# 39 rows of the gather stage get their dot products on TensorE

## The chip, the cores and the metric

One core of a Trainium2 chip runs the whole program: TensorE (matrix products, transposes), VectorE, ScalarE, GpSimd ("Pool", which here issues the indirect transfers) and SyncE (which issues the other transfers), with 16 transfer engines behind the queues. The metric is the device time of one execution in microseconds, as a median of runs.

## The reference

One layer on 256 tokens of width 2048, all in float32: a mixer of block attention and gated linear attention, a cross attention over 256 memory tokens, and a feed-forward part made of single experts, each with a layer norm behind it. The change lies in the feed-forward part:

```python
q = (xt @ w_query).reshape(T, PEER_HEADS, 2, PEER_QUERY_DIM // 2)
s = jnp.einsum('thpd,hpnd->thpn', q, sub_keys).astype(jnp.float32)
s_top, i_top = lax.top_k(s, PEER_TOPK)
...
best, pos = lax.top_k(cand, PEER_TOPK)
expert_idx = jnp.take_along_axis(cand_idx, pos, axis=-1)
gates = jax.nn.softmax(best, axis=-1)
...
u = expert_down[idx]
h = jax.nn.gelu(jnp.einsum('td,thkd->thk', xc, u).astype(jnp.float32), approximate=False)
vsel = expert_up[idx]
return jnp.einsum('thk,thkd->td', (g * h).astype(x.dtype), vsel)
```

So each of 256 tokens picks 16 of 16384 experts in each of 8 heads. Of each expert it needs one row of 2048 numbers of the table `peer_u` (expert_down) for a dot product with the token, and one of `peer_v` (expert_up) for the weighted sum.

## The kernel before

The tokens are two halves, s = 0 and s = 1, of 128 tokens, one to a partition. For each half and each of 8 x 16 = 128 slots there is thus one "row" of work: an indirect transfer (`gather`, L660) that fetches for each of 128 tokens its own expert's row of `peer_u`, 128 x 2048 float32 or 1.049 MB, and then a dot product of each partition's row with its token (`dot` in `u_row`, L669): one VectorE operation over 128 x 2048 with an accumulator, which writes one column of `z`. The last part of the kernel handles `peer_v` another way for most slots: it streams the whole table through TensorE against a matrix of weights that is built from one-hot tiles (`one_hot`, `weigh_hot`, `build`), block by block of tokens (IB = 4 tokens to a block).

`KS = (128, 75)` says how many slots of each half are gathered in the gather stage: all 128 of s = 0 and the first 75 of s = 1, 203 rows. The other 53 slots of s = 1 are left to the last part of the kernel, whose order is written by hand and is not touched.

The gather stage (`run`, L895 to L928) goes head by head. `peer_scores(h0, 2, h2)` computes the queries of two heads on TensorE (L200, from four tiles of `peer_wq`, tag "wr", 1 MB each), ScalarE copies them (`pq`, L204), TensorE multiplies them with the keys (L574). `route(s, h)` (L606 to L650) is the selection of the 16 experts: chains of maximum, find and replace operations on VectorE, an index computation (L629 to L642), and a softmax of the gate (ScalarE's exponential at L647, VectorE's reciprocal at L649). `gather_u(s, heads)` then issues a head's 16 gathers and dots; `weigh` (L684, L685) applies the Gelu and the gates to a head's 16 columns of `z`. In s = 1 the builds of 64 blocks run between the heads: for one block `one_hot` and `weigh_hot` write one-hot tiles (four VectorE operations of 128x128 at L744, called hot-row operations here, the rest on ScalarE at L731 and L733), TensorE multiplies them (L753), and ScalarE copies the result out (L756).

A gather needs a free slot. For s = 0 there are nine: three of the pool `g`, two halves of `h2s`, and four of `gslots`; for s = 1 there are six: three of `g` and three buffers "gw" of the tag "wr", which held the weight tiles before. A slot is free when the dot that reads it has run, so Pool's next gather waits for an earlier dot. The transfers then run on the queue of Pool.

There are two kinds of PSUM banks: `pp` (five) and `pa` (three). The order of the instructions in this stage isn't written out by hand: a scheduler sets the order of each engine from the priorities (the order in which the program is written) and from its own estimate of when each operand is ready. `tc.issue_after(x)` binds what is written under it to come after instruction x.

Of the kernel before, what the change touches and what calls it, by code (L numbers as in the profile page):

```python
# [7 lines left out]
F32 = mybir.dt.float32  # L8
# [4 lines left out]
ALU = mybir.AluOpType  # L13
# [3 lines left out]
P = 128  # L17
T = 256
D = 2048
KT = 16  # L20
# [5 lines left out]
PH = 8  # L26
NK = 128
TK = 16
# [23 lines left out]
TB = 4  # L52
LNC = ((0, 2, 0, 2), (0, 2, 0, 2))
SG = 8


class Body:
# [477 lines left out]
    def sub_keys(self):  # L535
        nc = self.nc
        src = self.A["peer_sub_keys"][0].rearrange("h s n d -> n (h s) d")
        self.skT = self.sm.tile([P, 2 * PH, P], F32, name="skT", bufs=1)
        tiles = []
        for g in range(4):  # L540
            t = self.sm.tile([P, 4, P], F32, name=self.name("sk"), tag="f2", bufs=4)
            nc.sync.dma_start(t, src[:, g * 4:(g + 1) * 4, :])
            tiles.append(t)
        self.sk_finish(self.sk_transpose(tiles[:2], "pa"))
        return tiles[2:]
# [107 lines left out]
    def gather(self, table, s, i):  # L653
# [8 lines left out]
            in_offset=bass.IndirectOffsetOnAxis(ap=self.eidx[:, s, i:i + 1], axis=0))  # L662
        return g

    def u_row(self, s, i):
        g = self.gather(self.A["peer_u"][0], s, i)

        def dot():
            self.nc.vector.scalar_tensor_tensor(g, g, 1.0, self.h2n[:, s, :], op0=ALU.mult, op1=ALU.mult,  # L669
                                                accum_out=self.z[:, s, i:i + 1])  # L670
        return dot

    def v_row(self, s, i):
# [13 lines left out]
    def gather_u(self, s, heads):  # L687
        for h in heads:
            lo, hi = h * TK, min((h + 1) * TK, KS[s])
            for i in range(lo, hi):  # L690
                self.u_row(s, i)()
            self.weigh(s, lo, hi)

    def residual(self):
# [149 lines left out]
    def run(self):  # L844
        A, nc, tc, ctx = self.A, self.nc, self.tc, self.ctx
# [25 lines left out]
        with tc.tile_pool(name="smR", bufs=2) as self.sm:  # L871
# [10 lines left out]
            h2 = h2s[:, 0:2, :].rearrange("p a (k t) -> p (a k) t", t=T)  # L882
# [14 lines left out]
            self.slots = spare  # L897
            self.gather_u(0, (0,))
            self.slots = spare + [lambda k=k: gs[:, k, :] for k in range(4)]
            todo = [(1,)]  # L900
            for h0 in (2, 4, 6):
                self.peer_scores(h0, 2, h2)
                for h in (h0, h0 + 1):
                    self.route(0, h)
                self.gather_u(0, todo.pop(0))
                todo.append((h0, h0 + 1))
            for h in range(2):
                self.route(1, h)
            self.gather_u(0, todo.pop(0))
# [104 lines left out]
```

## Time and profile before

| | us |
|---|---|
| median of 3 runs | 2262.85 (2260.82 to 2269.27) |
| the profiled execution | 2258.22 |
| its span in the trace | 2256.5 |
| VectorE busy in the span | 1717.4 |
| TensorE busy in the span | 1748.3 |

The trace is of one execution, and a sum over its rows is held against that execution's own 2258.22 us. In the gather stage the rows are numbered here 0 to 127 (s = 0) and 128 to 202 (s = 1), in order of their gathers; the first dot of row 48, which is head 3 of s = 0, starts at 1020.13 us, the first of s = 1 at 1248.82, and the last of them ends at about 1473.7. Heads are given as (s, head): head (0, 3) to (0, 7), then (1, 0) to (1, 4), whose last has 11 rows.

In rows of instructions the columns are the start and the duration in us, the engine, the line, the operation, output and inputs by the program's names, shapes, how many in a run, and in brackets the idle time ahead with what ended it. "PEclk" is TensorE's clock as granted, as a share of 2.4 GHz (0.50 is 1.2 GHz).

### The profile page before, as it was taken

The page shows a single profiled execution, that of the slowest core. Times are in us where ns is not written, and L with a number is a line of the kernel's source. Part 1 is how long each engine was busy: PE and PEld are TensorE (multiplying, and loading weights), DVE is VectorE, ACT ScalarE, POOL GpSimd, SP SyncE. Part 2 cuts the span into 40 slices and gives each one's busy share as a digit, 9 for nine tenths or more (in the row PEclk, how much of TensorE's full clock was granted, in tenths as well). Part 3 has the DMA queues.
Part 4 walks back from the last instruction along what each step waited for, and adds up shares of the span by engine and source line. Part 5 has one row for each costly group of instructions (what it writes and reads, how often), then busy time and mean ns, then how long its engine had stood idle before and what let it go on. Part 6 is the DMA issues. An engine that isn't in the chain of part 4 may idle for free.

```text
span 2256.5 us, 22663 instructions
## 1 busy us (share of the span) xinstructions
PE 1748.3 (77%) x8238; PEld 1454.3 (64%) x8238; DVE 1717.4 (76%) x2382; ACT 905.0 (40%) x1408; POOL 493.4 (22%) x348
## 2 busy tenths in 40 slices
PE   8999999899999979840000551069999999999995
PEld 7778887788888868630000440068888887888884
DVE  5456555754444458989999999898888887899886
ACT  4554544444444431203100561074444444444443
POOL 0000000100000004522376336901222221222211
PEclk9999999999999989875555555589999999999998
DMA  6554558455545729999999999959999998999992
GB/s 226 176 162 156 168 168 279 136 195 192 188 148 192 254 96 375 422 376 322 312 379 383 337 314 332 395 185 326 355 375 373 361 356 326 378 386 362 363 377 93
DMA packets 160783, 637.47 MB, mean 283 GB/s; under 512 B 12304, under 2 KB 24720, under 8 KB 103968
## 3 DMA queue, kind: packets, MB, share of 16 engines
q1 hardware_dynamic: 116176, 312.01, 38.9%
q0 software_dynamic: 44496, 324.03, 37.8%
q8 instruction: 64, 1.05, 0.2%
q14 instruction: 47, 0.39, 0.0%
HBM read 628.65 MB, written 7.34 MB: 282 GB/s over the span
## 4 chain that ended last, share of the span: by engine, by line
PE 68%; DVE 20%; DMA 6%; issue 4%; POOL 2%; ACT 1%; SPq 0%; ACTq 0%; DVEq 0%; POOLq 0%
PE pp L183 9%; PE pp L819 6%; PE pp L821 6%; PE pp L818 6%; PE pp L218 6%; PE pp L219 6%; PE pp L217 5%; PE pp L185 5%; DVE g L669 5%; PE pa L821 4%; PE pa L819 4%; PE pa L818 4%; DMA wr<-in_peer_wq_dram 3%; DVE oh L744 3%; DVE gslots L669 3%
## 5 line engine op out<-in xcount | busy, mean ns | idle before, releaser
L152 DVE TENSOR_TENSOR wl<-wr,wh 128x1024 fp32r<-128x1024 f32 x512 | 623.1, 1227 | 411.0 <-ACT wh L151 410.7
L151 ACT CAST wh<-wr 128x1024 fp32r<-128x1024 f32 x512 | 537.8, 1052 | 692.3 <-PE pa L821 347.5
L669 DVE SCALAR_TENSOR_TENSOR g<-g,y 128x2048 f32<-128x2048 f32 x138 | 316.6, 2304 | 12.2 <-DMA g<-in_peer_u_dram,eidx 12.2
L660 POOL DMA_INDIRECT g<-in_peer_u_dram,eidx x138 | 208.9, 1514 | 425.7 <-DVE g L669 343.6
L819 PE MATMUL pp<-wl,ah 128*128 128x512 f32 x640 | 251.8, 393 | 2.6 <-DVE wl L152 2.6
L818 PE MATMUL pp<-wh,ah 128*128 128x512 f32 x640 | 250.5, 391 | 3.6 <-issue 2.8
L821 PE MATMUL pp<-wh,al 128*128 128x512 f32 x640 | 209.8, 393 | 0.0
L720 PE MATMUL pa<-ident,w 128*128 128x128 f32 x2 | 0.9, 462 | 209.0 <-DVE w L685 209.0
L819 PE MATMUL pa<-wl,ah 128*128 128x512 f32 x384 | 150.1, 391 | 0.0
L818 PE MATMUL pa<-wh,ah 128*128 128x512 f32 x384 | 150.0, 391 | 0.0
L819 PEld LDWEIGHTS pp<-wl,ah 128*128 128x128 f32 x640 | 120.6, 188 | 30.7 <-DVE wl L152 4.1
L818 PEld LDWEIGHTS pp<-wh,ah 128*128 128x128 f32 x640 | 120.4, 188 | 30.7 <-issue 2.9
L821 PEld LDWEIGHTS pp<-wh,al 128*128 128x128 f32 x640 | 120.5, 188 | 25.9
L183 PE MATMUL pp<-x,wh 128*128 128x512 f32 x384 | 136.3, 398 | 0.0
L720 PEld LDWEIGHTS pa<-ident,w 128*128 128x128 f32 x2 | 0.4, 183 | 209.7 <-DVE w L685 205.1
L660 POOL DMA_INDIRECT g<-in_peer_v_dram,eidx x53 | 72.7, 1372 | 263.9 <-DVE y L678 235.0
L821 PE MATMUL pa<-wh,al 128*128 128x512 f32 x384 | 129.6, 392 | 0.0
L720 PE MATMUL pa<-ident,ij 128*128 128x128 f32 x4 | 1.3, 434 | 161.3 <-DVE ij L641 161.3
L678 DVE SCALAR_TENSOR_TENSOR y<-g,w,y 128x2048 f32<-128x2048 f32 x53 | 124.4, 2347 | 0.0
L669 DVE SCALAR_TENSOR_TENSOR gslots<-gslots,y 128x2048 f32<-128x2048 f32 x48 | 109.7, 2301 | 0.0
L185 PE MATMUL pp<-x,wl 128*128 128x256 f32 x384 | 108.5, 283 | 0.0
L200 PE MATMUL pp<-h2s,wr 128*128 128x256 f32 x384 | 92.0, 401 | 17.6 <-DMA wr<-in_peer_wq_dram 17.6
(293 smaller groups left out, 3708.3 us busy)
## 6 DMA issues: line engine op xcount, KB each, us to landing
wr<-in_peer_v_dram SPq DMA_DIRECT2D x128, 1024.0 KB, 7.6
wr<-in_w_in_dram SPq DMA_DIRECT2D x48, 1024.0 KB, 5.1
wr<-in_xattn_wkv_dram SPq DMA_DIRECT2D x32, 1024.0 KB, 5.3
wr<-in_w_out_dram SPq DMA_DIRECT2D x16, 1024.0 KB, 5.2
wr<-in_xattn_wq_dram SPq DMA_DIRECT2D x16, 1024.0 KB, 4.9
wr<-in_xattn_wo_dram SPq DMA_DIRECT2D x16, 1024.0 KB, 4.9
wr<-in_peer_wq_dram SPq DMA_DIRECT2D x12, 1024.0 KB, 16.9
spill<-stg SPq DMA_DIRECT2D x16, 320.0 KB, 2.8
```

The lines of the kernel that those rows point to most:

```text
L151: self.nc.scalar.copy(wh, raw)
L152: (eng or self.nc.vector).tensor_tensor(wl, raw, wh.bitcast(F32), op=ALU.subtract)
L183: nc.tensor.matmul(ps[j], wh[:, k, c], xhl[:, k0 + k, :], start=(first and k == 0), stop=False, skip_group_check=True)
L185: nc.tensor.matmul(ps[j][:, :T], wl[:, k, c], xhl[:, k0 + k, 0:T], start=False, stop=(last and k == WK - 1), skip_group_check=True)
L218: nc.tensor.matmul(ps[h], xh, wl[:, k, :], start=False, stop=False)
L219: nc.tensor.matmul(ps[h], xl, wh[:, k, :], start=False, stop=(last and k == WK - 1))
L660: self.nc.gpsimd.indirect_dma_start(out=g, out_offset=None, in_=table, in_offset=bass.IndirectOffsetOnAxis(ap=self.eidx[:, s, i:i + 1], ax ...
L669: self.nc.vector.scalar_tensor_tensor(g, g, 1.0, self.h2n[:, s, :], op0=ALU.mult, op1=ALU.mult, accum_out=self.z[:, s, i:i + 1])
L678: self.nc.vector.scalar_tensor_tensor(acc, g, self.w[:, s, i:i + 1], acc, op0=ALU.mult, op1=ALU.add)
L818: nc.tensor.matmul(o, ah[th], wh[:, c, :], start=first, stop=False)
L819: nc.tensor.matmul(o, ah[th], wl[:, c, :], start=False, stop=False)
L821: nc.tensor.matmul(out[th][cp * WK + c], al[th], wh[:, c, :], start=False, stop=last)
```

## The change

In heads (0, 3) to (0, 7) the rows with i % 16 in (1, 4, 7, 10), and in heads (1, 0) to (1, 4) those with i % 16 in (0, 4, 8, 11), no longer get a dot on VectorE: 20 + 19 = 39 rows. The row is gathered as before. Then (`pe_row`) TensorE transposes its 16 pieces of 128x128 in four groups of four into a `pa` bank, ScalarE copies each group to a tile `gT` (two buffers), and TensorE multiplies each transposed piece with the same piece of the transposed tokens and adds over the 16 pieces in a `pp` bank: 16 float32 products of 128x128x128. The bank then holds the product of every token with every token's expert row; the wanted dots are its diagonal. VectorE takes that by a 128x128 operation with the identity and the accumulator (L685 after). This operation is bound behind the dot of a row three or more later, or of the head's last row.

For s = 1 the transposed tokens have to outlast `h2`, since its buffer becomes one of the next stage's; ScalarE copies the half to `h2b`, in the buffer of the keys `skT`, which get a tag for it. The diff:

```diff
 SG = 8
+PD = ((1, 4, 7, 10), (0, 4, 8, 11))
+PD0 = 3
+PL = 3
...
         src = self.A["peer_sub_keys"][0].rearrange("h s n d -> n (h s) d")
-        self.skT = self.sm.tile([P, 2 * PH, P], F32, name="skT", bufs=1)
+        self.skT = self.sm.tile([P, 2 * PH, P], F32, name="skT", tag="skT", bufs=1)
         tiles = []
...
+    def pe_row(self, s, i):
+        nc = self.nc
+        g = self.gather(self.A["peer_u"][0], s, i)
+        out = self.bank()
+        for c in range(4):
+            ps = self.bank("pa")
+            for j in range(4):
+                k = 4 * c + j
+                nc.tensor.transpose(ps[:, j * P:(j + 1) * P], g[:, k * P:(k + 1) * P], self.ident)
+            gT = self.sm.tile([P, 4, P], F32, name=self.name("gT"), tag="gT", bufs=2)
+            nc.scalar.copy(gT, ps.rearrange("p (a t) -> p a t", a=4))
+            for j in range(4):
+                k = 4 * c + j
+                nc.tensor.matmul(out[:, :P], gT[:, j, :], self.h2T[s][:, k, :], start=k == 0, stop=k == KT - 1)
+
+        def diagonal():
+            dg = self.sm.tile([P, P], F32, name=self.name("dg"), tag="s0", bufs=2)
+            nc.vector.scalar_tensor_tensor(dg, out[:, :P], 1.0, self.ident, op0=ALU.mult, op1=ALU.mult,
+                                           accum_out=self.z[:, s, i:i + 1])
+        return diagonal
+
     def u_row(self, s, i):
...
         def dot():
-            self.nc.vector.scalar_tensor_tensor(g, g, 1.0, self.h2n[:, s, :], op0=ALU.mult, op1=ALU.mult,
-                                                accum_out=self.z[:, s, i:i + 1])
+            return self.nc.vector.scalar_tensor_tensor(g, g, 1.0, self.h2n[:, s, :], op0=ALU.mult, op1=ALU.mult,
+                                                       accum_out=self.z[:, s, i:i + 1])
         return dot
...
             lo, hi = h * TK, min((h + 1) * TK, KS[s])
+            pend = []
             for i in range(lo, hi):
-                self.u_row(s, i)()
+                if i % TK in PD[s] and (s, h) >= (0, PD0):
+                    pend.append((i + PL, self.pe_row(s, i)))
+                    continue
+                dot = self.u_row(s, i)()
+                while pend and (pend[0][0] <= i or i == hi - 1):
+                    with self.tc.issue_after(dot.ins):
+                        pend.pop(0)[1]()
             self.weigh(s, lo, hi)
...
             self.slots = spare + [lambda k=k: gs[:, k, :] for k in range(4)]
+            self.h2T = [h2[:, :, 0:P], None]
             todo = [(1,)]
...
                 todo.append((h0, h0 + 1))
+            h2b = self.sm.tile([P, KT, P], F32, name="h2b", tag="skT", bufs=1)
+            nc.scalar.copy(h2b, h2[:, :, P:T])
+            self.h2T[1] = h2b
             for h in range(2):
```

The 203 gathers keep their order on Pool, and SyncE's order stays. The order of the other engines is set anew. In the pieces below pp, pa are PSUM banks with a running number, ident the identity, gslots, g, gw, h2s slots of gathered rows or `h2`, wr a weight tile, oh the one-hot tiles, dg the diagonal's output.

TensorE where the scores of heads 6 and 7 of s = 0 are computed, before: the queries follow the scores of heads 4 and 5 at once.

```order
L574 MATMUL pa_6975<-skT,pq_6883 128x128 x2
L200 MATMUL pp_7149<-h2s,wr_7147 128x256 x8
L200 MATMUL pp_7158<-h2s,wr_7147 128x256 x8
L200 MATMUL pp_7149<-h2s,wr_7167 128x256 x8
L200 MATMUL pp_7158<-h2s,wr_7167 128x256 x8
```

And after, the same place: the last of head 3's four rows ends in it (L676 transposes, L681 products).

```order
L681 MATMUL pp_7266<-h2s,gT_7283 128x128 x4
L676 MATMUL pa_7289<-ident,gslots 128x128 x2
L676 MATMUL pa_7300<-ident,gslots 128x128 x4
L203 MATMUL pp_7333<-h2s,wr_7331 128x256
L681 MATMUL pp_7266<-h2s,gT_7294 128x128 x4
L681 MATMUL pp_7266<-h2s,gT_7305 128x128 x4
L203 MATMUL pp_7333<-h2s,wr_7331 128x256 x7
L203 MATMUL pp_7342<-h2s,wr_7331 128x256 x8
```

The queries of heads 6 and 7 (L203 is L200 of before) have moved behind the four rows of head 3.

TensorE in head 2 of s = 1, before: nothing but products of one-hot tiles, one block after the other.

```order
L720 MATMUL pa_7578<-ident,w 128x128
L753 MATMUL pp_7687<-oh_7677 128x128 x4
L753 MATMUL pa_7704<-oh_7694 128x128 x4
L753 MATMUL pp_7721<-oh_7711 128x128 x4
L753 MATMUL pp_7738<-oh_7728 128x128 x4
```

After, the same engine from the third group of that head's last row on (L784 is L753 of before):

```order
L676 MATMUL pa_9546<-ident,g_9510 128x128 x4
L784 MATMUL pp_9585<-oh_9575 128x128
L681 MATMUL pp_9512<-h2b,gT_9540 128x128 x4
L681 MATMUL pp_9512<-h2b,gT_9551 128x128 x4
L784 MATMUL pp_9585<-oh_9575 128x128 x3
L784 MATMUL pa_9602<-oh_9592 128x128 x4
L784 MATMUL pp_9619<-oh_9609 128x128 x4
L784 MATMUL pa_9636<-oh_9626 128x128 x4
L784 MATMUL pp_9653<-oh_9643 128x128 x4
L784 MATMUL pp_9670<-oh_9660 128x128 x4
L784 MATMUL pa_9687<-oh_9677 128x128 x4
L676 MATMUL pa_9740<-ident,gw_9737 128x128 x4
```

The builds of seven blocks now stand together between the head's last row and the next head's first.

VectorE in the same head, before: after each dot one block's four hot-row operations.

```order
L669 SCALAR_TENSOR_TENSOR g_7854,z<-g_7854,y 128x2048
L744 TENSOR_SCALAR oh_8203<-iota_91,ijT,wT 128x128 x4
L669 SCALAR_TENSOR_TENSOR gw_7857,z<-gw_7857,y 128x2048
L744 TENSOR_SCALAR oh_8313<-iota_91,ijT,wT 128x128 x4
L669 SCALAR_TENSOR_TENSOR gw_7860,z<-gw_7860,y 128x2048
```

After, the end of that head (L693 is the dot, L775 the hot-row operation, L709 the gates):

```order
L693 SCALAR_TENSOR_TENSOR g_9557,z<-g_9557,y 128x2048
L685 SCALAR_TENSOR_TENSOR dg_9560,z<-pp_9459,ident 128x128
L693 SCALAR_TENSOR_TENSOR g_9562,z<-g_9562,y 128x2048
L775 TENSOR_SCALAR oh_9677<-iota_91,ijT,wT 128x128 x4
L693 SCALAR_TENSOR_TENSOR gw_9565,z<-gw_9565,y 128x2048
L685 SCALAR_TENSOR_TENSOR dg_9568,z<-pp_9512,ident 128x128
L644 TENSOR_REDUCE ij<-eq_9725 128x2x16
L775 TENSOR_SCALAR oh_9971<-iota_91,ijT,wT 128x128
L693 SCALAR_TENSOR_TENSOR gw_9570,z<-gw_9570,y 128x2048
```

The four operations of the head's seventh block (oh_9677) stand between its dots, ahead of the last row's diagonal (pp_9512); the next head's blocks (oh_9971 and on) begin behind it.

## Rows read from the trace of the kernel before

**Rows 1.** The page's slices: the span in 40 equal parts of 56.4 us each.

```profile
PEclk9999999999999989875555555589999999999998
DMA  6554558455545729999999999959999998999992
```

**Rows 2.** Stretches: us, busy PE, PEld, VectorE, ScalarE, Pool, PEclk, transfers, GB/s; then L669 alone.

```profile
904.00:959.00 55.00, 44.58 (x195) 37.78 (x194) 55.00 (x137) 10.73 (x28) 31.08 (x21) 0.89 1.02 422
...
1248.80:1356.40 107.60, 62.71 (x238) 53.42 (x239) 107.17 (x193) 66.80 (x194) 32.67 (x34) 0.50 0.92 323
1356.40:1473.70 117.30, 5.47 (x22) 4.24 (x20) 107.93 (x123) 8.38 (x22) 86.78 (x42) 0.50 0.95 369
1020.10:1473.70 453.60, 69.32 (x261) 58.14 (x261) 443.59 (x730) 104.55 (x297) 243.70 (x157) 0.50 0.93 348
...
988.20:1020.10 31.90, 22.83 (x20) 0.54 0.88 325
...
1020.10:1473.70 453.60, 357.20 (x310) 0.50 0.93 348
```

**Rows 3.** VectorE's waits, 1020.1 to 1473.7: in all, times, longest.

```profile
DVE g L669 <- DMA g<-in_peer_u_dram,eidx: 5.4, 10, 1.8
DVE gw L669 <- DMA gw<-in_peer_u_dram,eidx: 2.8, 5, 1.9
```

**Rows 4.** VectorE's instructions in order, in head 0 of s = 1.

```profile
1252.06 2.28 DVE L669 SCALAR_TENSOR_TENSOR g<-g,y 128x2048 f32<-128x2048 f32 x1
...
1254.27 1.34 DVE L744 TENSOR_SCALAR oh<-iota,ijT,wT 128x128 f32<-128x128 f32 x4
1255.31 2.28 DVE L669 SCALAR_TENSOR_TENSOR g<-g,y 128x2048 f32<-128x2048 f32 x1
```

**Rows 5.** Pool's issue of a gather at two places.

```profile
1062.03 0.94 POOL L660 DMA_INDIRECT g<-in_peer_u_dram,eidx  x1 [2.48 <-DVE mr L611]
...
1201.83 1.91 POOL L660 DMA_INDIRECT g<-in_peer_u_dram,eidx  x1 [0.30 <-issue]
```

**Rows 6.** The wait before 988.3, single instructions; then landing times of weight tiles, 840 to 1000.

```profile
988.28 0.16 DVE L649 RECIPROCAL gr<-gs 128x1 f32<-128x1 f32 x1 [10.61 <-ACT gate L647]
...
982.29 0.59 ACT L204 COPY pq<-pp 128x512 f32<-128x512 f32 x1 [19.88 <-PE pp L200]
...
978.54 7.17 PE L200 MATMUL pp<-h2s,wr 128*128 128x256 f32 x32 [2.64 <-DMA wr<-in_peer_wq_dram]
...
DMA to landing us min/median/max: 11.5/19.9/28.1
```

**Rows 7.** Two groups: ns min, median, max; then in all and mean ns, idle ahead.

```profile
L407 DVE TENSOR_TENSOR s<-pa,causal_add x8: 283/291/292, 245.1 to 341.6; 128x128 f32<-128x128 f32 x8
...
L279 ACT COPY h2s<-pa 128x512 f32<-128x512 f32 x4 | 2.3, 586 | 8.0 <-PE pa L275 8.0
```

**Rows 8.** TensorE's instructions at full clock (first, last) and at half.

```profile
818.58 1.03 PE L553 MATMUL pp<-ident,sk 128*128 128x128 f32 x8
...
1469.63 0.66 PE L720 MATMUL pa<-ident,ij 128*128 128x128 f32 x2 [106.15 <-DVE ij L641]
1474.58 0.45 PE L720 MATMUL pa<-ident,w 128*128 128x128 f32 x1 [4.29 <-DVE w L685]
1475.95 2.08 PE L753 MATMUL pp<-oh 128*128 128x128 f32 x8 [0.92 <-DVE oh L744]
1477.82 1.61 PE L753 MATMUL pa<-oh 128*128 128x128 f32 x8
...
1489.91 2.19 PE L753 MATMUL pp<-oh 128*128 128x128 f32 x16 [0.46 <-DVE oh L744]
```

**Rows 9.** TensorE about 850 us, and the stretch from 850 to 852.

```profile
847.96 1.22 PE L200 MATMUL pp<-h2s,pw 128*128 128x256 f32 x2 [0.67 <-ACT h2s L279]
...
848.98 2.45 PE L275 MATMUL pa<-ident,y 128*128 128x128 f32 x12
...
850.00:852.00 2.00, 2.00 (x13) 1.72 (x12) 0.74 (x1) 1.66 (x3) 1.59 (x2) 0.77 0.19 78
```

## The prediction

> **What bounds the kernel now.** I read the page's slices first, then busy time by stretch, then what each engine waited for there, then single rows. In the slices [rows 1] TensorE's clock sits at half from about 1015 to 1467 us, and the transfer engines show 9 tenths. That is the gather stage, and the edit lies in it. By stretch [rows 2], VectorE is busy 443.6 of the 453.6 us between 1020.1 and 1473.7, in which rows 48 to 202 are consumed (310 records, two to a dot); TensorE is busy 69. VectorE waited for data only 5.4 + 2.8 us there [rows 3]. A dot starts 2.21 us before the next operation [rows 4], so 155 dots are 343 us, and about 101 us of its time is other work: the selection of experts, and the four hot-row operations (1.04 us) per block. So VectorE bounds most of the stage, but a second bound lies close under it. From 1356.4 to 1473.7 it is busy 107.9 of 117.3 us, the transfers stand at 0.95, and 43 rows take 117.3 us: 2.73 us a row. A row is 1.049 MB; at the 422 GB/s of the best stretch, 904 to 959 us, where the transfers stand at 1.02, it is 2.5 us. And Pool's issue of one gather takes 0.94 us when it falls between dots and 1.91 us when dots follow each other [rows 5], so that a dense run of dots also slows the issue.
>
> One wait ahead of row 48 matters: VectorE stands 10.6 us until 988.3 for a gate on ScalarE, which itself sat 19.9 us behind the query copies of heads 6 and 7 [rows 6]. TensorE computed those scores there, and its weights came 11.5 to 28.1 us after their issue.
>
> **The change, part by part.**
>
> Removed from VectorE: 39 dots, 39 x 2.21 = 86.2 us. Added to it: 39 diagonals. The nearest row is a 128x128 operation reading PSUM, 0.29 us [rows 7]; the lower end is one hot-row operation, 0.26, the upper end 0.7 with the accumulator's read and a late product. I take 0.30: 11.7 us. VectorE's net: -74.5 us (-59 to -76).
>
> Added to TensorE, per row: 16 transposes and 16 products (one product is two records in the trace). At half clock two transposes take 0.66 us and one 0.45, so one costs 0.21; four products take 1.87 us from one group's start to the next, 0.47 each. At full clock: 1.03 / 8 = 0.13 and 2.19 / 8 = 0.27 [rows 8]. A row is 10.9 us at half and 6.4 us at full clock. Which clock? A row is one dense run, and the clock rose at about 850.9 us (0.77 on the mean from 850 to 852) inside a run that from 848.98 us on was twelve transposes [rows 9]. I take the first 4 us of a row at half and the rest at full: 8 us, less where rows follow closely. The Trainium skill ("TensorE: Matmul & The Clock Gate", Part 4: PE-mode transpose) says that the full clock does not engage for transposes, which would speak against this change. By that rule a row would stay near 10.9 us; the trace disagrees at 850.9 us, though one product, two records, stood at its head [rows 9].
>
> Added to ScalarE: four 128x512 copies a row, 4 x 0.59 us [rows 7], 92 us in all. It is busy 105 of the 453.6 us [rows 2], and the copies of a row overlap the next group's transposes, so I charge nothing; where a copy queues behind a one-hot build, TensorE waits for it, and that is in the 8 us. The copy of h2's second half runs once, off the path.
>
> Moved: the order is rebuilt. Two places matter. First, on TensorE the scores of heads 6 and 7 now stand behind the four rows of head 3 (the first piece of order in the section on the change). So the 10.6 us wait goes. From 988.2 to 1020.1 VectorE ran ten dots and 9 us of selection [rows 2]; 5.6 us of that, of later heads, now stand behind head 3, which so starts at about 1004 instead of 1020. Later VectorE comes to head 6's selection after three dots of head 4, at 1004 + 25.6 + 6.6 = 1036. But head 3's last PE row, row 58, lands eleven rows after row 47, the last that nine slots let Pool issue by 985: at about 1013. TensorE ends it at 1020, needs four weight tiles at 7.17 us = 28.7, and from a tile's end to VectorE's release it took 2.6 us (985.7 to 988.3) [rows 6]: 1051. The fourth weight tile is issued only when the first is used; I add 3 to 4 us. VectorE waits from 1036 to 1055. The slots fill meanwhile, so the transfers lose little. Second, in the gathers of s = 1 the blocks' builds come seven at a time at each head's end. VectorE's seventh set of hot rows waits for a buffer that the first build frees, which stands behind the head's last PE row (the second and third piece); 5 us a head, which VectorE's slack covers, as the sum shows. TensorE's own sum for such a head is 4 x 8 + 7 x 1.1 to 1.9 = 40 to 45 us. That is close to the transfers; without that closeness it would cost nothing.
>
> VectorE's work by head after, from the new order (12 dots, 4 diagonals, and the other work that now stands there): heads 3 to 7 of s = 0: 26, 47, 56, 38, 27; heads 0 to 4 of s = 1: 42, 36, 36, 36, 23. In all 367; 443.6 + 5.6 moved in - 74.5 is 375, and records that overlap a little explain the rest.
>
> The sum. s = 0: 1055 + the remaining 40 of head 4 + 56 + 38 + 27 = 1216, and 5 for small waits: 1221, against 1248.8. That is -28. Between its ends: no wait at 1036 (1202, -47), or 15 us more of it (1236, -13). s = 1: VectorE's 173 us are under the transfers now. 75 rows at 2.5 us are 188; at 2.73, the rate of the old last stretch, 205. Fewer dots free Pool, and the bundles of builds hold a slot longer; I take 2.7: 203, against 1473.7 - 1248.8 = 224.9. That is -22 (-37 to -10). The end: the last head's four builds and the last PE row now stand ahead of the transposition of w on TensorE: +3. Sum: -28 - 22 + 3 = **-47 us**. The profiled execution took 2258.2 us (span 2256.5); -47 gives 2211. The median of the runs is 2262.85, 4.6 us above it, so the forecast is **2216 us**.
>
> **The rivals.**
>
> *TensorE at half clock becomes the bound, slower.* Each row has half its records in transposes and gaps between rows, and from 1248.8 to 1356.4 us TensorE is busy 62.7 of 107.6 us and the clock never rises [rows 2]. By the sentence of the Trainium skill above ("TensorE: Matmul & The Clock Gate", Part 4) it would be this. Row 49 lands at about 991; head 3's rows then end at 991 + 44 = 1035, the scores at full clock (dense products) at 1066, and four heads at 43.6 end at 1241, -8. A head of s = 1 takes 4 x 10.9 + 7 x 1.87 = 57 us, and all of them 4 x 57 + 40 = 268, +43. With the end +38: 2301 us by the median. It decides from the point where a PE row takes over 9.5 us, for 48 us is what 16 rows of s = 1 take now and the builds take 10. Against it: the rise at 850.9 us. Chance 0.10.
>
> *Transfers already bind, no change.* The transfer share is 0.93 over the whole stretch. For it: from 1356.4 on it carries only 369 GB/s at 0.95. Against it: the same share carries 323 GB/s where VectorE is full and 422 elsewhere [rows 2], and VectorE hardly waited [rows 3]. It would leave 5 us: 2258. Chance 0.08.
>
> *The new order costs more.* Head 6's scores come 15 us later still (weights at 28 us from issue), and s = 1 gains only 10: -13 - 10 + 3 = -20, 2243. Chance 0.17.
>
> *All overlaps.* TensorE keeps its full clock, rows go at 2.5 us, VectorE never waits at 1036: -47 - 37 + 3 = -81, 2182. Chance 0.12.
>
> **How the numbers follow.** My forecast, 2201 to 2232, has 0.53. The range should leave out at most 2 in 10: it drops the slow case and the unchanged one, 0.18, and reaches over the other three, so it runs from 2178 to 2254. About 0.5%, 11 us, is what a measurement can tell from no change. Faster by more: 0.53 + 0.17 + 0.12 = 0.82. Within: 0.08. Slower: 0.10.
>
> **What would show it.** In the profile after: the 10.6 us wait near 980 us is gone and a wait of 10 to 25 us for the score copies of head 6 stands at about 1036; the diagonal takes 0.25 to 0.35 us; TensorE's granted clock is mixed, 0.6 to 0.9, from 1000 us on; the last row of s = 0 lies near 1220 and the stage's end near 1427; VectorE waits for transfers or TensorE some 30 us in s = 1, and gathers are issued faster there. It is wrong if the clock stays at 0.50 and VectorE waits at the diagonals, or if the transfers carry under 380 GB/s in s = 1 with VectorE and TensorE both idle.

## The result: 2233.5 us, 29 less than before

The changed kernel takes 2233.51 us in the median of four runs (2230.32 to 2235.17), the kernel before 2262.72. The ratio is 0.9874, with an interval from 0.9857 to 0.9891; a second time, on another occasion, it was 0.9864 (0.9838 to 0.9891). By the ratios that is 28 to 31 us faster, inside the range of the prediction (2178 to 2254), 17.5 us above its forecast of 2216, and just above the 2201 to 2232 to which it gave 0.53. The profiled execution took 2235.17 us, with a span of 2233.5.

The slices of its page, in the same order as [rows 1]: VectorE's busy tenths, TensorE's granted clock, the transfers.

```profile
DVE  5456556754444548995998887788888878889886
PEclk9999999999999998859878888899999999999998
DMA  6544457455644738999889999859999998999992
```

The clock, at half through the whole stage before, now stands at 0.75 to 0.91 of full on the mean of a head. By stretch, in the columns of [rows 2], heads (0, 3) to (0, 7) one by one, then these five together and the gathers of s = 1:

```profile
998.84:1033.10 34.26, 32.37 (x220) 29.79 (x221) 28.22 (x37) 9.01 (x18) 25.38 (x16) 0.91 1.01 427
1033.10:1094.57 61.47, 49.33 (x310) 43.57 (x308) 43.52 (x116) 17.68 (x36) 28.62 (x16) 0.91 0.83 325
1094.57:1149.96 55.39, 28.51 (x192) 26.26 (x192) 55.32 (x182) 16.34 (x45) 33.91 (x21) 0.75 0.94 368
1149.96:1187.38 37.42, 27.50 (x190) 25.90 (x191) 37.28 (x82) 12.33 (x26) 22.85 (x13) 0.86 0.89 333
1187.38:1230.45 43.07, 29.85 (x209) 27.00 (x208) 34.35 (x61) 22.74 (x55) 30.02 (x18) 0.82 1.01 426
...
998.84:1230.45 231.61, 167.55 (x1117) 152.52 (x1118) 198.69 (x472) 78.10 (x178) 140.78 (x82) 0.85 0.93 371
1230.45:1441.50 211.05, 157.34 (x1155) 146.16 (x1153) 169.24 (x302) 104.35 (x277) 143.27 (x77) 0.88 0.94 369
```

VectorE, which was busy in 443.6 of 453.6 us before, is busy in 198.7 of 231.6 and in 169.2 of 211.0. The transfers kept their share (0.93 and 0.94). Heads 3 and 7 of s = 0 run at 426 and 427 GB/s with VectorE idle for a part, head 5 at VectorE's rate, and head 4 at neither: there both have gaps.

Cut at the first dots of heads on VectorE, at the last gates and at the first product of the last stage, the two spans differ like this.

| stretch | before | after | forecast | measured |
|---|---|---|---|---|
| to the first dot of the stage | 851.3 | 848.5 | 0 | -2.7 |
| heads (0, 0) to (0, 2) | 168.9 | 150.3 | -16 | -18.6 |
| heads (0, 3) to (0, 7) | 228.7 | 231.6 | -12 | +2.9 |
| s = 1, to the last gates | 225.5 | 211.0 | -22 | -14.4 |
| last builds | 48.4 | 51.2 | +3 | +2.8 |
| last stage | 733.9 | 740.8 | 0 | +7.0 |
| span | 2256.5 | 2233.5 | -47 | -23.0 |

One cut is not the same in both. Row 128, the first of s = 1, is one of TensorE's in the changed kernel, so the first dot there is row 129's. From the last gates of s = 0 to that dot are 4.4 us, in the kernel before 1.0: 3.4 us of s = 1 stand in the line above it. With them put back, heads (0, 3) to (0, 7) are at -0.5 and s = 1 is at -11.0. The same holds for every kernel below that has TensorE's rows in s = 1.

So the gain ahead of head 3 came, the one behind it in s = 0 did not, and s = 1 gave half. The +7 of the last stage, where nothing is changed, is dealt with at the end.

Where heads (0, 3) to (0, 7) lost theirs can be seen at one place. These are TensorE (queries of heads 6 and 7 at L203, then head 4's first transposes at L676), ScalarE, VectorE and Pool, one after the other in the trace's timeline:

```profile
1025.83 20.45 PE L203 MATMUL pp<-h2s,wr 128*128 128x256 f32 x94
1048.15 8.86 PE L203 MATMUL pp<-h2s,wr 128*128 128x256 f32 x32 [1.86 <-DMA wr<-in_peer_wq_dram]
1056.85 2.00 PE L577 MATMUL pa<-skT,pq 128*128 128x128 f32 x16
...
1053.59 0.59 ACT L207 COPY pq<-pp 128x512 f32<-128x512 f32 x1 [20.62 <-PE pp L203]
...
1057.94 0.49 DVE L610 MAX8 val<-sc 128x8 f32<-128x128 f32 x2 [14.38 <-ACT sc L583]
...
1058.68 1.47 PE L676 MATMUL pa<-ident,gslots 128*128 128x128 f32 x12
...
1064.47 0.94 POOL L663 DMA_INDIRECT gslots<-in_peer_u_dram,eidx  x1 [25.80 <-PE pa L676]
```

And two windows of 6 us there:

```profile
1054.00:1060.00 6.00, 6.00 (x42) 5.55 (x41) 2.06 (x14) 2.90 (x7) 0.00 (x0) 1.00 0.29 124
1060.00:1066.00 6.00, 4.17 (x35) 3.78 (x34) 6.00 (x29) 5.02 (x10) 1.23 (x2) 1.00 0.00 0
```

TensorE finished head 3's rows at 1025.8 and went on with the queries and scores of heads 6 and 7, four weight tiles in 33 us. VectorE had head 6's selection next in its order from 1043.6 us on, and waited 14.4 us for those scores, until 1057.9. Behind the scores stood head 4's first transposed row. It held its slot until it was transposed, after 1058.7, and Pool, whose next gather wanted that slot, issued nothing for 25.8 us. What was queued ran out: the transfers fell to 0.29 and then to nothing. Heads 5 and 6 went at VectorE's rate. In head 7, with 27 us of work by the forecast (30 in the trace, up to the last gates), VectorE could have caught up; but there the transfers were the limit, at 1.01.

In s = 1 a smaller form of it returns at each head's start. TensorE, ScalarE, Pool and VectorE at head 1:

```profile
1270.34 1.46 PE L676 MATMUL pa<-ident,gw 128*128 128x128 f32 x9 [2.94 <-DMA gw<-in_peer_u_dram,eidx]
1273.97 3.78 PE L681 MATMUL pp<-h2b,gT 128*128 128x128 f32 x16 [2.17 <-ACT gT L678]
1277.54 1.14 PE L676 MATMUL pa<-ident,gw 128*128 128x128 f32 x7
...
1269.46 1.35 ACT L762 ACTIVATE oh<-iota,ijT 128x128 f32<-128x128 f32 x4
1271.35 1.28 ACT L708 ACT_TABLE_LOAD   x1
1273.35 0.56 ACT L678 COPY gT<-pa 128x512 f32<-128x512 f32 x1
...
1278.96 2.42 POOL L663 DMA_INDIRECT gw<-in_peer_u_dram,eidx  x1 [4.96 <-PE pa L676]
...
1296.72 2.29 DVE L693 SCALAR_TENSOR_TENSOR g<-g,y 128x2048 f32<-128x2048 f32 x1 [3.65 <-DMA g<-in_peer_u_dram,eidx]
```

The row landed at 1270.3. Its first copy stood on ScalarE behind one-hot tiles (L762) and the Gelu with its table load (L708) until 1273.4, its last transposes ran at 1278, Pool waited 5.0 us for the slot, and VectorE found no row at 1293: 3.65 us. Such waits of Pool for a "gw" slot, over s = 1 (in all, times, longest):

```profile
POOL gw L663 <- PE pa L676: 31.3, 6, 7.9
```

A second thing stands beside it, and the prediction had it the other way round ("gathers are issued faster there"). Pool's time in their issue, before (L660) and after (L663; stretch, us, Pool busy with gathers, clock, transfers, GB/s):

```profile
1248.82:1473.70 224.88, 108.95 (x71) 0.50 0.94 347
1230.45:1441.50 211.05, 135.40 (x72) 0.88 0.94 369
```

The mean issue went from 1.53 to 1.88 us. In a version below, where the dots have 16 columns, it is 0.94: it is the issue beside wide dots that takes long, as in [rows 5]. In the changed kernel 25 of the 72 took over 2.15 us right behind another one, so that Pool itself was slower there than a transfer's 2.45 us, by 14 us in all (5.6 before). How much of s = 1 goes to this and how much to the held slots no run separates.

### The profile page after: what moved, and what is told of

It reads as the page before. It is cut to its first block, busy times and chain, and to the rows that moved or that the text cites. A ratio compares the mean times of both kernels' runs of the same rounds, so it can differ in the third digit from the quotient of the medians.

```text
span 2233.5 us, 26708 instructions
## 1 busy us (share of the span) xinstructions
PE 1978.9 (89%) x10110; PEld 1670.4 (75%) x10110; DVE 1636.5 (73%) x2382; ACT 982.6 (44%) x1565; POOL 543.6 (24%) x348
## 4 chain that ended last, share of the span: by engine, by line
PE 69%; DVE 18%; DMA 5%; issue 3%; ACT 3%; POOL 2%; SPq 0%; ACTq 0%; DVEq 0%; POOLq 0%
PE pp L186 9%; PE pp L850 6%; PE pp L852 6%; PE pp L849 6%; PE pp L221 6%; PE pp L222 6%; PE pp L220 6%; PE pp L188 5%; PE pa L852 4%; PE pa L849 4%; PE pa L850 4%; DVE g L693 4%; DVE gslots L693 3%; PE pp L681 2%; DVE oh L775 2%
## 5 line engine op out<-in xcount | busy, mean ns | idle before, releaser
L663 POOL DMA_INDIRECT g<-in_peer_u_dram,eidx x138 | 228.4, 1655 | 388.0 <-DVE g L693 332.4
L693 DVE SCALAR_TENSOR_TENSOR g<-g,y 128x2048 f32<-128x2048 f32 x125 | 285.9, 2294 | 29.6 <-DMA g<-in_peer_u_dram,eidx 29.6
L678 ACT COPY gT<-pa 128x512 f32<-128x512 f32 x156 | 85.6, 588 | 145.7 <-PE pa L676 144.7
L663 POOL DMA_INDIRECT g<-in_peer_v_dram,eidx x53 | 72.6, 1369 | 264.1 <-DVE y L702 239.7
L681 PE MATMUL pp<-h2s,gT 128*128 128x128 f32 x640 | 92.4, 303 | 40.3 <-ACT gT L678 39.4
L681 PEld LDWEIGHTS pp<-h2s,gT 128*128 128x128 f32 x640 | 84.1, 212 | 50.3 <-ACT gT L678 50.3
L681 PE MATMUL pp<-h2b,gT 128*128 128x128 f32 x608 | 91.8, 312 | 28.4 <-ACT gT L678 27.7
L681 PEld LDWEIGHTS pp<-h2b,gT 128*128 128x128 f32 x608 | 83.8, 221 | 38.0 <-ACT gT L678 38.0
```

Of the source, the lines that this page charges most:

```text
L663: self.nc.gpsimd.indirect_dma_start(out=g, out_offset=None, in_=table, in_offset=bass.IndirectOffsetOnAxis(ap=self.eidx[:, s, i:i + 1], ax ...
L681: nc.tensor.matmul(out[:, :P], gT[:, j, :], self.h2T[s][:, k, :], start=k == 0, stop=k == KT - 1)
L693: return self.nc.vector.scalar_tensor_tensor(g, g, 1.0, self.h2n[:, s, :], op0=ALU.mult, op1=ALU.mult, accum_out=self.z[:, s, i:i + 1])
```

## The experiments

For each kernel the ratio to the kernel before, and the same cuts (us):

| kernel | ratio (interval) | (0, 0)-(0, 2) | (0, 3)-(0, 7) | s = 1 | builds | last stage |
|---|---|---|---|---|---|---|
| before | 1 | 168.9 | 228.7 | 225.5 | 48.4 | 733.9 |
| changed | 0.9874 (0.9857-0.9891) | 150.3 | 231.6 | 211.0 | 51.2 | 740.8 |
| a2_changed_again | 0.9864 (0.9838-0.9891) | 149.7 | 229.0 | 210.9 | 51.2 | 734.6 |
| e1_s0_only | 0.9899 (0.9874-0.9924) | 149.4 | 228.5 | 224.4 | 48.4 | 741.8 |
| e2_s1_only | 0.9990 (0.9973-1.0007) | 174.1 | 232.1 | 216.0 | 51.2 | 734.6 |
| e3_short_dots | 0.9821 (0.9793-0.9848) | 169.8 | 204.0 | 207.1 | 48.4 | 747.7 |
| e3b_work_beside | 1.0066 (1.0041-1.0091) | 156.6 | 259.0 | 226.5 | 48.4 | 735.3 |
| e4_scores_first | 0.9888 (0.9863-0.9913) | 170.1 | 212.0 | 210.1 | 51.2 | 735.1 |
| e5_builds_spread | 0.9939 (0.9918-0.9960) | 150.6 | 232.4 | 228.2 | 48.8 | 740.4 |
| e7_gate_first | 0.9972 (0.9954-0.9990) | 164.9 | 228.7 | 226.6 | 48.4 | 742.7 |
| e8_both_first | 0.9846 (0.9816-0.9876) | 163.2 | 212.1 | 211.6 | 51.2 | 735.4 |
| e9_no_wait | 0.9855 (0.9827-0.9883) | 162.9 | 212.8 | 211.5 | 51.2 | 743.4 |
| e10_from_head2 | 0.9852 (0.9826-0.9878) | 176.3 | 207.2 | 213.8 | 51.2 | 735.2 |
| e11_floor | 0.9803 (0.9770-0.9837) | 168.8 | 193.0 | 221.5 | 48.8 | 731.7 |

**The two halves.** One tuple emptied each time:

```diff
-PD = ((1, 4, 7, 10), (0, 4, 8, 11))
+PD = ((1, 4, 7, 10), ())
...
+PD = ((), (0, 4, 8, 11))
```

> The changed kernel with TensorE's rows in s = 0 alone (20 rows; all 75 rows of s = 1 get VectorE dots again). Theory A, from the two traces: the change gains 18 us ahead of head (0, 3) (order of the scores), loses 3 in heads (0, 3) to (0, 7), gains 14 in s = 1, and the end's builds cost 3. So this kernel keeps -15 and its s = 1 takes about 225 us as before: ratio about 0.993, some 2247 us. Theory B, that the 39 rows count alike wherever they lie: 20/39 of the 28.5 us, 2248 us; the trace tells them apart: by A heads (0, 3) to (0, 7) still take about 230 us, by B about 215.

> The changed kernel with TensorE's rows in s = 1 alone (19 rows). Theory A: s = 0 runs as before, with the 10.6 us wait for the gate near 988 and heads (0, 3) to (0, 7) in about 229 us; s = 1 takes about 211 us, the end's builds 3 more than before: -14 + 3, some 2252 us, ratio 0.995. If TensorE's slower spacing in the last stage (0.233 against 0.229 us per product, +7 us) comes of a busy TensorE in the gather stage, it shows here too; if it is chance, not.

The first measured 2238.42 us, the second 2258.43. By either theory the 20 rows of s = 0 should have given some 15 us; they gave 21, more than either, and the trace puts it where theory A does: heads (0, 3) to (0, 7) in 228.5 us with 20 dots fewer on VectorE, all the gain ahead of them. The rows of s = 1 alone give nothing that can be told from zero: 9.5 us in s = 1, 2.8 back in the builds, and 8.6 us more in s = 0, where the edit has no rows. Of these 8.6, 5.2 lie ahead of head 3, where the wait for the gate was 15.1 us in this trace, not 10.6; the other 3.4 are the later cut, and belong to s = 1, which so gains 6.1. The two halves do not add up to the whole: 21 and 1 us alone, 28 to 31 together.

**The relief without the work.** In the kernel before, 39 dots over 16 columns:

```diff
+            n = 16 if i % TK in PD[s] and (s, i // TK) >= (0, PD0) else D
-            self.nc.vector.scalar_tensor_tensor(g, g, 1.0, self.h2n[:, s, :], op0=ALU.mult, op1=ALU.mult,
+            self.nc.vector.scalar_tensor_tensor(g[:, :n], g[:, :n], 1.0, self.h2n[:, s, :n], op0=ALU.mult, op1=ALU.mult,
```

> The kernel before, with the same 39 dots cut to 16 of 2048 columns (2032 columns of these products are left out) and no work on TensorE: what VectorE's relief alone gives. Theory A (in the changed kernel slots are held by TensorE's rows, and the transfers stop for it): without them rows go at 2.5 to 2.6 us, and 155 rows take about 395 to 405 us instead of 453.6; 2263 - 50 - 5 = about 2210 us. Theory C (the transfers of these rows run at about 2.8 us a row whatever frees the slots, as in the changed kernel: 155 x 2.85 = 442): about 2245 us. The 10.6 us wait near 988 stays in both.

2221.19 us, 38 less. VectorE's work falls by 39 x 2.21 = 86 us, less what the short operations take; 42 us of it show in the cuts. Heads (0, 3) to (0, 7), then heads 0, 1 and 3 of s = 1:

```profile
1021.00:1224.90 203.90, 1.14 (x3) 0.47 (x3) 186.17 (x416) 29.18 (x82) 125.21 (x81) 0.50 0.97 386
...
1224.94:1279.88 54.94, 34.11 (x177) 30.45 (x178) 54.02 (x132) 48.60 (x151) 16.29 (x17) 0.72 0.93 353
1279.88:1321.67 41.79, 14.07 (x81) 12.83 (x80) 41.21 (x89) 19.34 (x56) 21.69 (x14) 0.66 0.85 306
...
1363.80:1403.38 39.58, 0.00 (x0) 0.00 (x0) 29.00 (x36) 0.22 (x1) 31.28 (x18) 0.50 1.01 427
```

In s = 0 the transfers stand at 0.97, 2.55 us a row, as theory A had it. In s = 1 the mean is 2.76, near theory C's figure and the changed kernel's 2.81 (2.86 with the 3.4 us put back), but it is a mean of two different things. In heads 0 and 1 VectorE is busy 54.0 of 54.9 and 41.2 of 41.8 us: in this kernel all the builds of s = 1 lie there, as nearly all do in the kernel before (32 blocks of four tokens; the 64 and IB given ahead are wrong), and VectorE still bounds. In heads 2 to 4 it has slack, and 43 rows take 110.4 us, 2.57 a row, with the transfers at 1.01 and 417 to 427 GB/s. So theory C, a slow row whatever frees the slots, is out.

Against this kernel the changed one, with the 3.4 us put back, is 7 us longer in s = 1, and in s = 0 (from the first dot on) 2 to 5. That is not the price of the added work alone: the changed kernel has seven builds in each head instead of all in the first two, and by head its s = 1 takes 48.2, 46.9, 45.1, 44.5, 29.7 us, here 54.9, 41.8, 42.1, 39.6, 28.7. Taken as it is, of the 50 us that the forecast had for the two halves 42 come with the dots merely cut (the wait for the gate still in them), and 30 to 34 with the work on TensorE: 8 of what is missing were not to be had by this relief at all, and 9 to 12 went with the added work and its order. The limit shows wherever VectorE is relieved: in head 7 of s = 0, too, the transfers stand at 1.01 with 428 GB/s. Then the floor, every dot from head 3 on cut:

```diff
-            n = 16 if i % TK in PD[s] and (s, i // TK) >= (0, PD0) else D
+            n = 16 if (s, i // TK) >= (0, PD0) else D
```

> The kernel before, with every dot from head 3 on cut to 16 of 2048 columns (the rest of these products is left out): the floor that the transfers set. Theory A (transfers at 422 to 428 GB/s where nothing stops them): 2.5 us a row, heads (0, 3) to (0, 7) about 200 us and s = 1 about 188 us. Rival (a gather in s = 1, with six slots and beside the builds, has 2.76 us a row of its own, as with 39 short dots): s = 1 stays at about 205 us.

2217.76 us (ratio 0.9803, 0.9770 to 0.9837), hardly less than with 39 short dots. Heads (0, 3) to (0, 7) take 193.0 us; s = 1 takes 221.5, more than either theory's 188 and 205. By head that is 70.7, 42.0, 39.3, 39.4, 30.2. From heads (1, 2) and (1, 3), where no build runs:

```profile
1310.00:1390.00 80.00, 0.00 (x0) 0.00 (x0) 8.43 (x70) 2.15 (x5) 34.91 (x37) 0.50 1.01 426
```

Pool's gathers follow each other at 2.45 us there, with the same six slots, so six slots alone do not make a row of s = 1 longer. Beside the builds, the rival's other condition, no run shows such a floor: in heads 0 and 1 VectorE waited 28 us for builds and 14 for a copy on ScalarE, and the transfers stood at 0.74 and 0.79. What binds there is not taken apart.

**The work without the relief.** All dots stay, and the transposes read the tokens instead of the row:

```diff
-        g = self.gather(self.A["peer_u"][0], s, i)
+        g = self.h2n[:, s, :]
...
-                                           accum_out=self.z[:, s, i:i + 1])
+                                           accum_out=self.tiny.tile([P, 1], F32, name=self.name("gz"), tag="gz"))
...
                     pend.append((i + PL, self.pe_row(s, i)))
-                    continue
```

> All 203 dots on VectorE, and beside them the transposes, copies, products and diagonals of 39 rows, made of the tokens in place of gathered rows (so that they wait for no transfer and hold no slot; their results go to a spare column). It prices the added work alone. Theory A (the work itself is cheap, holding slots and the place in TensorE's order is what costs): VectorE gains 39 x 0.26 = 10 us, ScalarE and TensorE hide the rest: 2263 + 10 + 3 = about 2276 us. Rival (ScalarE's copies delay gates, Gelus and one-hot tiles): 2295 us or more.

2278.54 us, 16 more, as theory A said, but not only for its reason. s = 1 takes 1 us more, so 19 rows of such work, when they wait for no transfer and hold no slot, are hidden there. In s = 0, 12 us are gained ahead of head 3 and 30 lost behind it, and VectorE's longest wait from 940 us on shows half of why:

```profile
DVE val L610 <- ACT sc L583: 15.6, 1, 15.6
```

The scores of heads 6 and 7 stand late on TensorE in this kernel too. Twenty diagonals of 0.26 us are another 5 us of the 30; the rest is not traced. The gain ahead of head 3 and the wait behind it are two ends of one move.

**The scores.** Their place moved back, ahead of head 3's rows; then, in the kernel before, ScalarE's copies bound behind head 5's gate; then both:

```diff
                 self.peer_scores(h0, 2, h2)
+                if h0 == 6:
+                    self.gather_u(0, (3,))
...
-                todo.append((h0, h0 + 1))
+                todo.append((h0,) if h0 == 2 else (h0, h0 + 1))
...
-                    self.nc.scalar.copy(dst[:, 2 * b:2 * b + 2, :], ps[b].rearrange("p (a t) -> p a t", a=2))
+                    with self.tc.issue_after(self.late.ins) if self.late else ExitStack():
+                        self.nc.scalar.copy(dst[:, 2 * b:2 * b + 2, :], ps[b].rearrange("p (a t) -> p a t", a=2))
```

> The changed kernel with the queries and scores of heads 6 and 7 written ahead of head 3's gathers, so that TensorE has them ahead of the first transposed row, as in the kernel before. Theory A (what s = 0 loses in the changed kernel comes of head 4's first transposed row standing behind these scores on TensorE: Pool waits 25.8 us for its slot from 1038 to 1064, the transfers stop from about 1057 to 1065, and VectorE waits 14.4 us for the scores): the three waits go, heads (0, 3) to (0, 7) fall from 231.6 to about 205 us, as with the shortened dots; the 10.6 us wait for the gate near 985 returns, so heads (0, 0) to (0, 2) take 167 again instead of 150. Net some -8 to -10: 2225 us. Theory B (TensorE's rows hold their slots too long wherever the scores stand): heads (0, 3) to (0, 7) stay above 225 us and the wait near 985 is added: about 2245 us.

> The kernel before, all dots on VectorE, with ScalarE's copies of the queries of heads 6 and 7 bound behind head 5's gate, so that VectorE need not wait 10.6 us for that gate near 988. Theory A: VectorE bounds the rest of the stage, so these 10 us are kept to the end: heads (0, 0) to (0, 2) take about 158 us, (0, 3) to (0, 7) 229; 2250 us. Rival: the wait only moves to the selection of head 6 or to a transfer later, and the time stays within 3 us of before.

> Both edits on the changed kernel: scores of heads 6 and 7 ahead of head 3's gathers, and their copies bound behind head 5's gate. Theory A: neither wait is left; heads (0, 0) to (0, 2) 155 to 160 us, (0, 3) to (0, 7) about 205 us, s = 1 211: about 2215 us, faster than the changed kernel by some 18. Theory B: 2235 us.

2236.91, 2255.91 and 2228.39 us. With the scores first, heads (0, 3) to (0, 7) fall by 20 us, and heads (0, 0) to (0, 2) take 20 more. VectorE's wait for the gate is back, and Pool's longest wait for a slot held for TensorE is 7.3 us instead of 25.8 (columns: in all, times, longest), so its theory B is out:

```profile
DVE gr L652 <- ACT gate L650: 12.1, 1, 12.1
...
POOL gslots L663 <- PE pa L676: 18.6, 6, 7.3
```

The mechanism is thus as theory A has it, the size of the net wrong: nothing is gained, where 8 to 10 us were expected. Binding the copies gives 6.3 us in the kernel before by the ratio (2 to 10 by its interval; 4.0 in the cut of heads (0, 0) to (0, 2)) where 10 were expected: most of the wait only moved, as the rival had it, to a copy of head 5's positions on ScalarE (`abf`), 6.3 us. The same wait is left in the version with both:

```profile
DVE eq L641 <- ACT abf L636: 6.5, 1, 6.5
```

Two further steps: the copies bound behind head 5's abf copy as well, then also the rows of TensorE from head 2 on.

```diff
-                self.late = self.gated if h0 == 6 else None
+                self.late = (self.abf, self.gated) if h0 == 6 else None
...
-PD0 = 3
+PD0 = 2
...
-                    self.gather_u(0, (3,))
+                    self.gather_u(0, (2, 3))
...
-                todo.append((h0,) if h0 == 2 else (h0, h0 + 1))
+                todo.append(() if h0 == 2 else (h0, h0 + 1))
```

> As the version with both edits (scores of heads 6 and 7 ahead of head 3's gathers, their copies behind head 5's gate), and the copies also behind the copy of head 5's positions (abf), for which VectorE waited 6.5 us there. Theory A: heads (0, 0) to (0, 2) fall from 163 to about 157 us, the rest stays (212, 211): 2222 us. Rival: as each time so far the wait moves on (to the scores of head 6 in head 4): 2228 us.

> That version with the rows of TensorE from head 2 on (43 instead of 39) and the scores of heads 6 and 7 ahead of head 2's rows. By VectorE's work alone: 4 x 1.95 = 8 us less, 2214 us, for in heads 0 to 2 VectorE and not the transfers binds (3.5 us a row). Theory A says no gain: head 2's rows land from about 950 on, but stand on TensorE behind scores whose weights come at about 980; they hold their slots, Pool and then VectorE wait 10 us or more: 2225 us or slower.

2230.39 and 2229.63 us. In the first the rival was right, the wait has moved on to the scores of head 6:

```profile
988.73 0.30 DVE L613 MAX8 val<-sc 128x8 f32<-128x128 f32 x1 [4.68 <-ACT sc L586]
```

In the second, four more rows came off VectorE and nothing was gained. VectorE waited for the scores, and Pool for a transposed row behind them, at the place that theory A named (VectorE from 961 to 1030, Pool from 961 to 1100):

```profile
DVE val L613 <- ACT sc L586: 14.5, 1, 14.5
...
POOL g L666 <- PE pa L679: 31.9, 2, 27.9
```

Beside these two, on the same chip, the changed kernel took 2230.32 us (0.9864, 0.9838 to 0.9891); the version with both, on another chip, has 0.9846 (0.9816 to 0.9876). So none of these three orders can be told from it; a version that is clearly faster was not found.

**The builds.** In s = 1 a block's build written behind every second or third row instead of seven at a head's end:

```diff
+                if more:
+                    more(i)
...
-                self.gather_u(1, (h,))
-                while b < HB and b * KS[1] < (h + 1) * TK * HB:
-                    self.one_hot(b)
-                    self.weigh_hot(b)
-                    self.build(b)
-                    b += 1
+                self.gather_u(1, (h,), blocks)
+            blocks(KS[1])
```

> The changed kernel with the 32 blocks of s = 1 written between the rows (a block behind every second or third row) instead of seven at each head's end. Theory A (ScalarE's copies of a transposed row queue behind the one-hot tiles of seven blocks, 4 us at each head's start, so the row holds its slot, Pool waits 5 to 8 us and the transfers pause): s = 1 falls from 211 to about 200 us, 2222 us. Theory C (transfers bind at 2.8 us a row): s = 1 stays at 208 to 213 us, 2233 us.

2247.88 us: s = 1 took 17 us more than in the changed kernel, against either theory. VectorE's and TensorE's longest waits in s = 1:

```profile
DVE oh L777 <- PE pp L786: 29.1, 8, 4.6
DVE oh L777 <- PE pa L786: 16.4, 5, 4.6
...
PE pp L681 <- ACT gT L678: 56.6, 18, 7.4
```

A hot-row operation needs the buffer that an earlier build frees. Spread out, each build stands on TensorE behind the products of a row, which wait 56.6 us in all for ScalarE's copies (27.7 in the changed kernel); these stand behind one-hot tiles and Gelus, which wait 17.6 us for VectorE's dots and diagonals; and VectorE waits 45.5 us for the builds, where in the changed kernel it never did. Read together, three engines, each in its own order, wait in a ring. Seven at a head's end are the better order, though a copy on ScalarE is late by 2 to 4 us there.

**The changed kernel again.**

> The changed kernel once more, beside the next three on one chip. 2234 us, ratio 0.986 to 0.989. TensorE's spacing in the last stage, 0.233 us (216 products in 50 us) in its first trace, is 0.229 (220) in half of the other traces, with and without rows on TensorE; if that is a matter of the single execution, this trace may show either, and the last stage is 734 or 741 to 748 us accordingly.

2230.32 us, and a last stage of 734.6 us where the first trace has 740.8; the other cuts agree within 2.6 us.

## Why the prediction was right, and where it was not

- **VectorE bounds, and 39 dots less relieve it: right, with a limit I saw and did not put into the sum.** The 39 diagonals took 0.285 us each, and the next operation of VectorE started 0.26 after one (0.30 taken). As a group (in all, mean ns, idle ahead):

```profile
L685 DVE SCALAR_TENSOR_TENSOR dg<-pp,ident 128x128 f32<-128x128 f32 x39 | 11.1, 285 | 0.0
```

- **TensorE's rows: right where they follow each other.** The four groups of a row in head 3, two in a line, and the start of a row that came after a wait:

```profile
1013.18 1.04 PE L676 MATMUL pa<-ident,h2s 128*128 128x128 f32 x8
1014.51 2.05 PE L681 MATMUL pp<-h2s,gT 128*128 128x128 f32 x16 [0.29 <-ACT gT L678]
1016.39 1.04 PE L676 MATMUL pa<-ident,h2s 128*128 128x128 f32 x8
1017.72 2.05 PE L681 MATMUL pp<-h2s,gT 128*128 128x128 f32 x16 [0.29 <-ACT gT L678]
...
1091.60 1.94 PE L676 MATMUL pa<-ident,h2s 128*128 128x128 f32 x8 [6.13 <-DMA h2s<-in_peer_u_dram,eidx]
```

The stretches around these two places:

```profile
1006.90:1025.80 18.90, 17.87 (x148) 16.42 (x148) 13.64 (x19) 6.44 (x12) 13.00 (x9) 1.00 1.01 425
1091.50:1094.50 3.00, 1.94 (x8) 1.57 (x8) 3.00 (x10) 0.22 (x1) 2.77 (x1) 0.50 1.02 431
```

Two groups' transposes and products are 3.2 us from one to the next, so a row is 6.4 at full clock, as taken from [rows 8]. The row that came after 6.1 us of wait starts at half (0.24 us a transpose in place of 0.13; 0.21 had been taken). Of the 8 us charged for a row the first 4 were taken at half clock; no row of the trace before gave that length. The mean was 0.85 and 0.88 of full clock, and TensorE busy 167.6 of 231.6 and 157.3 of 211.0 us, so the slow rival is out. A row behind a wait can take longer than the 9.5 us from which it decides (the one at 1091.6 took 15, of which 4.5 behind a copy). By the rule of the Trainium skill on which that rival rested ("TensorE: Matmul & The Clock Gate", Part 4: PE-mode transpose) the clock should have stayed low in transposes; the stretch from 1006.9 to 1025.8 has 1.00, with the transposes always among products.
- **Ahead of head 3: right,** -18.6 for -16. The wait for the gate went, and so did the selection that moved.
- **The wait for head 6's scores: right in place and size,** 14.4 us until 1057.9 for 19 until 1055. The sentence behind it failed: "The slots fill meanwhile, so the transfers lose little." They had nothing queued for some 10 us. The scores' place is a matter of give and take: moved back, 20 us come back behind head 3 and 20 go ahead of it.
- **The rest of s = 0: the step that failed.** I added up VectorE's own work by head, 26, 47, 56, 38, 27 us, and beside the wait for the scores only 5 us for waits. Heads 4 to 6 came about as forecast; heads 3 and 7 took 34.3 and 39.7 us (43.1 to the later cut), since 16 rows need 16 x 2.45 = 39 us of transfers and nine slots can't store a head ahead. The bound that I had worked out, 2.5 us a row, was used in s = 1 alone. VectorE's own work was right: up to the last gates it was busy 194.3 us (194 taken). It was idle 32.9: 14.4 for the scores, and 18.5 where I had 5, 17 of them for rows that had not landed. (By head there is a slip: the 26 of head 3 should be 27.7 for 12 dots and 4 diagonals at my own prices.) This is 11 of the 20 us by which the measured cuts (without the last stage and the start) fall short of the forecast. Over the whole of s = 0 it makes -19 for -28.
- **s = 1: the mechanism right, the term too large,** and with it the rest of the 20: 214.4 us for 203 with the 3.4 us put back, 2.86 us a row for 2.7. VectorE was under the transfers, as forecast, but these ran at 369 GB/s. Two things that the sum had at nothing stand there: slots held at heads' starts, where a copy on ScalarE queues behind one-hot tiles (Pool waits 31.3 us for TensorE's transposes), and Pool's issue, which fewer dots did not free but which grew from 1.53 to 1.88 us. Their shares are open. The -10 that closes this term's range had no working behind it: 2.73 us a row gives -20, and the measured -11 would lie outside. That it lies inside is luck.
- **The end: right,** +2.8 for +3.
- **The rivals.** "Transfers already bind" is nearer than its 0.08: it holds in each stretch where VectorE is relieved, as in head 7. "The new order costs more" came closest in size (2243); one of its two reasons held, s = 1 gaining only 10 or so; the other, scores later still, did not: they came when forecast. The sign of being wrong that came nearest is the rate of s = 1, 369 GB/s where under 380 was named; but VectorE and TensorE were not both idle, they were busy 80 and 75%.

## What to carry to other kernels

When work is taken off an engine that bounds a stage, put the next bound into every stretch, not into the sum: a stretch takes the longer of the two, and a buffer of nine slots carries little from one to the next. A row that is consumed by an engine working in order holds its slot until everything ahead of it on that engine has run, so look for what waits there (here 33 us of score products) before moving rows to it. A wait that one can see ahead of a bound may be paid again behind it; its removal is worth what is left after both places are counted.

## What the runs showed of the hardware

The last stage, the same work in all kernels, runs at two rates while the granted clock is 1.00. TensorE's columns at two places of the changed kernel, of its second trace, and of the version without waits:

```profile
1500.00:1550.00 50.00, 50.00 (x216) 40.51 (x215) 43.24 (x44) 23.57 (x28) 10.05 (x8) 1.00 0.88 316
1900.00:1950.00 50.00, 50.00 (x220) 41.00 (x220) 43.75 (x36) 24.52 (x28) 10.73 (x8) 1.00 0.99 390
```

```profile
1500.00:1550.00 50.00, 50.00 (x220) 41.00 (x220) 44.23 (x45) 23.40 (x26) 10.65 (x9) 1.00 0.94 344
1900.00:1950.00 50.00, 50.00 (x221) 41.00 (x219) 43.74 (x36) 23.96 (x28) 10.75 (x8) 1.00 0.97 377
```

```profile
1500.00:1550.00 50.00, 50.00 (x220) 41.04 (x219) 43.73 (x45) 23.50 (x27) 10.10 (x8) 1.00 0.93 333
1900.00:1950.00 50.00, 50.00 (x216) 40.47 (x215) 43.92 (x36) 24.07 (x28) 10.08 (x8) 1.00 0.96 361
```

50 us hold 216 records or 220, 2% apart, for hundreds of us at a time; in the first trace the slow stretch is the first half of the stage, in the third the second half, in the second there is none. Of 14 traces six have such a stretch, with and without rows on TensorE, and it makes the last stage some 6 to 14 us longer. So the +7 us in the table are of the execution and not of the change; what sets the rate stays open. Profiles should be compared by stage for that reason, and a difference of two single spans of under some 10 us says nothing of a change.
